# A row-wise L1 normalization: five places of ten rows in one SBUF tile, and one 40 KB packet per partition and transfer

## The chip, the core and the metric

The kernel runs on one core of one Trainium2 chip. The metric is the device time of one launch in microseconds (us). The kernel before was run three times: median 316.6 us, from 316.41 to 316.69.

## What is computed

```python
def reference(x):                       # x: 32 x 512 x 1024, float32
    sums = np.sum(np.abs(x), axis=-1, keepdims=True)
    return (x / (sums + 1e-8)).astype(np.float32)
```

Each of the 32 x 512 = 16,384 rows of 1024 numbers is divided by the sum of its absolute values. A row is 4 KB. The whole input is 67.11 MB and has to be read from HBM once; the output is as large and has to be written once.

## The kernel before, in words

The chip's SBUF has 128 partitions, so each partition gets 128 rows in all. The work is cut into eleven tiles: ten of 12 rows per partition and a last one of 8 (`rows`, line 31). Tiles 0, 1 and the last are cut out of the first 32 rows of each partition's share of the head of the input (`HEAD`, lines 33 to 38), so that their partitions lie 32 rows (128 KB) apart in HBM; the other tiles are contiguous blocks in which the partitions lie 12 rows (48 KB) apart. Within a partition the rows of a tile are always contiguous in HBM and in SBUF.

The program order is written out by hand (`manual_schedule`, lines 108 to 115). There are four buffers of 12 rows per partition (`BUFS`, line 42). Four loads are issued first. Then, for each tile in turn: compute it, store it, and issue the load that will reuse its buffer, four tiles further on.

- **load** (lines 85 to 87) is one DMA issued on SyncE's queue (SP; queue q1 in the profile). It waits until the store that used the buffer before has landed.
- **compute** (lines 45 to 73, 103 to 106): VectorE (DVE) sums the absolute values of each row (L47), adds 1e-8 (L54) and takes the reciprocal (L56). Then the rows are scaled in place: most of them by one VectorE multiplication with the reciprocals broadcast along the row (L58), some by one VectorE instruction per row (L65), some by one ScalarE (ACT) instruction per row (L68). The table `split` (line 76) says how many: of tile 0, five rows go to L58, three to L65 and four to ScalarE; tiles 1 and 2 give three rows to ScalarE, the last but one gives it two, and the last has four for L65 and four for ScalarE.
- **store** (lines 89 to 101) is one or two DMAs issued on ScalarE's queue (queue q10), in ScalarE's program order.

`max_dma_last_dim` sets the longest contiguous run, in bytes, that becomes one packet of a DMA. Each tile's rows of a partition are cut into such packets: 48 KB (`WHOLE`) for the loads of tiles 0 and 1 and for the stores of the last two tiles, 24 KB (`HALF`) for nearly everything else, so two packets per partition. The store of tile 0 is in two DMAs: three rows in packets of 4 KB, then nine rows in packets of 36 KB. The store of tile 8 is in two DMAs of six rows.

The core has 16 DMA engines, and both queues use all of them.

Of the kernel before, what the change touches and what calls it, by code (L numbers as in the profile page):

```python
# [1 line left out]

# [4 lines left out]

FP32 = mybir.dt.float32
EPS = 1e-8


@with_exitstack
def kernel(
    ctx: ExitStack,
    tc: tile.TileContext,
    x: bass.AP,
    out: bass.AP,
):
    nc = tc.nc
    P = nc.NUM_PARTITIONS  # L20

    x_flat = x.flatten_outer_dims()
    out_flat = out.flatten_outer_dims()
    n, d = x_flat.shape

    R = 12
    BUFS = 4
    HEAD = 32
    per_partition = n // P
    assert n % P == 0 and (per_partition - HEAD) % R == 0  # L30
    rows = [R] * ((per_partition - HEAD) // R + 2) + [HEAD - 2 * R]

    def piece(flat, i):
        head = flat[: P * HEAD, :].rearrange("(p r) d -> p r d", p=P)
        if i < 2:
            return head[:, R * i : R * (i + 1), :]
        if i == len(rows) - 1:
            return head[:, 2 * R :, :]
        a = P * (HEAD + R * (i - 2))
        return flat[a : a + P * R, :].rearrange("(p r) d -> p r d", p=P)  # L40

    sbuf = ctx.enter_context(tc.tile_pool(name="sbuf", bufs=BUFS))
    stats = ctx.enter_context(tc.tile_pool(name="stats", bufs=len(rows)))

    def normalize(x_tile, k, kv, kt):
        s = stats.tile([P, R], FP32)
        nc.vector.tensor_reduce(  # L47
            out=s[:, :k],
            in_=x_tile[:, :k, :],
            axis=mybir.AxisListType.X,  # L50
            op=mybir.AluOpType.add,
            apply_absolute_value=True,
        )
        nc.vector.tensor_scalar_add(out=s[:, :k], in0=s[:, :k], scalar1=EPS)  # L54
        inv = stats.tile([P, R], FP32)
        nc.vector.reciprocal(out=inv[:, :k], in_=s[:, :k])  # L56
        if kv:
            nc.vector.tensor_mul(  # L58
                out=x_tile[:, :kv, :],
                in0=x_tile[:, :kv, :],  # L60
                in1=inv[:, :kv].unsqueeze(2).to_broadcast([P, kv, d]),
            )
        for r in range(kv, kv + kt):
            row = x_tile[:, r, :]
            nc.vector.tensor_scalar_mul(out=row, in0=row, scalar1=inv[:, r : r + 1])  # L65
        for r in range(kv + kt, k):
            row = x_tile[:, r, :]
            nc.scalar.activation(  # L68
                out=row,
                in_=row,  # L70
                func=mybir.ActivationFunctionType.Copy,
                scale=inv[:, r : r + 1],
            )

    last = len(rows) - 1
    split = {0: (3, 4), 1: (0, 3), 2: (0, 3), last - 1: (0, 2), last: (4, 4)}

    tiles = {}

    HALF, WHOLE = 24576, 49152
    FIRST = 3

    def load(i):
        x_tile = tiles[i] = sbuf.tile([P, R, d], FP32, name="x_tile")
        nc.sync.dma_start(out=x_tile[:, : rows[i], :], in_=piece(x_flat, i), max_dma_last_dim=WHOLE if i < 2 else HALF)  # L87

    def store(i):
        if i == 0:  # L90
            parts = [(0, FIRST, 4 * d), (FIRST, R, WHOLE)]
        elif i == last - 2:
            parts = [(0, R // 2, HALF), (R // 2, R, HALF)]
        else:
            parts = [(0, rows[i], WHOLE if i >= last - 1 else HALF)]
        for a, b, size in parts:
            nc.scalar.dma_start(
                out=piece(out_flat, i)[:, a:b, :],
                in_=tiles[i][:, a:b, :],
                max_dma_last_dim=size,  # L100
            )

    def compute(i):
        k = rows[i]
        kt, ks = split.get(i, (0, 0))
        normalize(tiles[i], k, k - kt - ks, kt)

    with tc.manual_schedule():
        for i in range(BUFS):
            load(i)  # L110
        for i in range(len(rows)):
            compute(i)
            store(i)
            if i + BUFS < len(rows):
                load(i + BUFS)


# [1 line left out]
_INS = ['x']  # L119
_OUTS = [((32, 512, 1024), 'float32')]  # L120


# [23 lines left out]
```

## Time and profile before

| what | value |
|---|---|
| time, median of 3 runs | 316.6 us (316.41 to 316.69) |
| span of the profiled execution, first to last instruction | 315.2 us |
| what a run's time holds beyond that span (median less span) | 1.4 us |
| VectorE busy | 260.6 us, 83% of the span, 50 instructions |
| ScalarE busy | 18.5 us, 6% |
| bytes moved | 134.22 MB, mean 426 GB/s over the span |
| DMA packets | 5761 |

The profiled execution has no time of its own beside its span; 1.4 us is what launch and end add to it, by the median. "Busy" of a queue is the time that its packets took, summed over the 16 DMA engines and divided by 16 spans. Packets under 512 B are the markers, one per DMA and engine, that report a transfer's end. A packet's bytes and its time are counted where it begins, so the rate of a short window is uneven.

### The profile page before, as it was taken

The page shows a single profiled execution, that of the slowest core. Times are in us where ns is not written, and L with a number is a line of the kernel's source. Part 1 is how long each engine was busy: PE and PEld are TensorE (multiplying, and loading weights), DVE is VectorE, ACT ScalarE, POOL GpSimd, SP SyncE. Part 2 cuts the span into 40 slices and gives each one's busy share as a digit, 9 for nine tenths or more (in the row PEclk, how much of TensorE's full clock was granted, in tenths as well). Part 3 has the DMA queues.
Part 4 walks back from the last instruction along what each step waited for, and adds up shares of the span by engine and source line. Part 5 has one row for each costly group of instructions (what it writes and reads, how often), then busy time and mean ns, then how long its engine had stood idle before and what let it go on. Part 6 is the DMA issues. An engine that isn't in the chain of part 4 may idle for free.

```text
span 315.2 us, 172 instructions
## 1 busy us (share of the span) xinstructions
DVE 260.6 (83%) x50; ACT 18.5 (6%) x17; POOL 0.2 (0%) x4
## 2 busy tenths in 40 slices
DVE  0079999999999999989996997999699969999000
ACT  0010503004000000000000000000000000203200
POOL 0000000000000000000000000000000000000000
DMA  8999999999999999999999999999999999999997
GB/s 318 480 399 412 437 407 464 411 436 413 415 446 437 415 446 437 415 449 434 415 449 437 412 449 437 412 449 437 415 446 437 415 437 434 432 428 496 399 408 324
DMA packets 5761, 134.22 MB, mean 426 GB/s; under 512 B 385, under 2 KB 385, under 8 KB 769
## 3 DMA queue, kind: packets, MB, share of 16 engines
q1 hardware_dynamic: 2736, 67.11, 49.8%
q10 hardware_dynamic: 3024, 67.11, 49.4%
q14 instruction: 1, 0.00, 0.0%
HBM read 67.11 MB, written 67.11 MB: 426 GB/s over the span
## 4 chain that ended last, share of the span: by engine, by line
DVE 40%; DMA 33%; another core or an unknown queue 18%; ACT 1%; issue 0%; SPq 0%
DVE s L47 23%; DMA x_tile<-in_x_dram 17%; DMA out_dram<-x_tile 16%; DVE x_tile L58 15%; ACT x_tile L68 1%; DVE x_tile L65 1%; DVE inv L56 0%; DVE s L54 0%; SPq L87 0%
## 5 line engine op out<-in xcount | busy, mean ns | idle before, releaser
L47 DVE TENSOR_REDUCE s<-x_tile 128x12 f32<-128x12288 f32 (+1 forms) x11 | 138.2, 12562 | 29.8 <-DMA x_tile<-in_x_dram 29.8
L58 DVE TENSOR_TENSOR x_tile<-x_tile,inv 128x12288 f32<-128x12288 f32 (+3 forms) x10 | 113.6, 11358 | 0.5
L68 ACT ACTIVATE x_tile<-x_tile,inv 128x1024 f32<-128x1024 f32 x16 | 17.2, 1138 | 256.9 <-DVE inv L56 256.9
L65 DVE TENSOR_SCALAR x_tile<-x_tile,inv 128x1024 f32<-128x1024 f32 x7 | 4.8, 749 | 0.0
L56 DVE RECIPROCAL inv<-s 128x12 f32<-128x12 f32 (+1 forms) x11 | 2.5, 226 | 0.4
L68 ACT ACT_TABLE_LOAD x1 | 1.3, 1283 | 17.8 <-DMA x_tile<-in_x_dram 17.8
L54 DVE TENSOR_SCALAR s<-s 128x12 f32<-128x12 f32 (+1 forms) x11 | 1.9, 174 | 0.4
L130 POOL MEMSET const-bfloat16-1.0<- 128x1 bf16 x1 | 0.1, 101 | 0.0
L130 POOL MEMSET const-uint8-127<- 128x1 uint8 x1 | 0.1, 101 | 0.0
L130 POOL MEMSET const-float32-0.0<- 128x1 f32 x1 | 0.1, 98 | 0.2 <-issue 0.2
L130 POOL MEMSET const-float32-1.0<- 128x1 f32 x1 | 0.1, 98 | 0.0
## 6 DMA issues: line engine op xcount, KB each, us to landing
x_tile<-in_x_dram SPq DMA_DIRECT2D x10, 6144.0 KB, 36.9
out_dram<-x_tile ACTq DMA_DIRECT2D x8, 6144.0 KB, 49.1
out_dram<-x_tile ACTq DMA_DIRECT2D x2, 3072.0 KB, 33.4
out_dram<-x_tile ACTq DMA_DIRECT2D x1, 4608.0 KB, 37.9
x_tile<-in_x_dram SPq DMA_DIRECT2D x1, 4096.0 KB, 32.2
out_dram<-x_tile ACTq DMA_DIRECT2D x1, 4096.0 KB, 20.9
out_dram<-x_tile ACTq DMA_DIRECT2D x1, 1536.0 KB, 29.3
```

Source lines behind the costliest of these rows:

```text
L47: nc.vector.tensor_reduce(out=s[:, :k], in_=x_tile[:, :k, :], axis=mybir.AxisListType.X, op=mybir.AluOpType.add, apply_absolute_value=True,)
L54: nc.vector.tensor_scalar_add(out=s[:, :k], in0=s[:, :k], scalar1=EPS)
L56: nc.vector.reciprocal(out=inv[:, :k], in_=s[:, :k])
L58: nc.vector.tensor_mul(out=x_tile[:, :kv, :], in0=x_tile[:, :kv, :], in1=inv[:, :kv].unsqueeze(2).to_broadcast([P, kv, d]),)
L65: nc.vector.tensor_scalar_mul(out=row, in0=row, scalar1=inv[:, r : r + 1])
L68: nc.scalar.activation(out=row, in_=row, func=mybir.ActivationFunctionType.Copy, scale=inv[:, r : r + 1],)
L130: nc = _bacc.Bacc("TRN2", target_bir_lowering=False, num_devices=1)
```

## The change

- Tiles have 10 rows instead of 12 (twelve tiles of 10 and a last one of 8), all cut from the input in order; the head of 32 rows is gone.
- The buffers are five places of 10 rows in one tile `x_all` of 50 rows per partition, instead of four buffers of 12 rows. `cell(i, a, b)` names rows a to b of tile i's place. Five loads are issued first instead of four.
- `max_dma_last_dim` is 40,960 bytes for every DMA but one, so that each load and each store has one packet per partition (40 KB; 32 KB for the last tile). The exception is the first row of tile 0, stored by a DMA of its own in packets of 4 KB; the other nine rows follow in one of 36 KB packets.
- The scaling is split otherwise: VectorE's one multiplication takes all ten rows of tiles 1 to 11. ScalarE takes five rows of tile 0 and four of the last.

The diff, without the lines that only rename a tile (in `compute`, `x_tile[:, ...]` becomes `cell(i, ...)`):

```diff
-    R = 12
-    BUFS = 4
-    HEAD = 32
+    R, SLOTS = 10, 5
+    PACKET = 40960
     per_partition = n // P
-    rows = [R] * ((per_partition - HEAD) // R + 2) + [HEAD - 2 * R]
+    rows = [R] * (per_partition // R) + [per_partition % R] * (per_partition % R > 0)
+    last = len(rows) - 1
+    split = {0: (0, 5), last: (4, 4)}
 
     def piece(flat, i):
-        head = flat[: P * HEAD, :].rearrange("(p r) d -> p r d", p=P)
-        if i < 2:
-            return head[:, R * i : R * (i + 1), :]
-        if i == len(rows) - 1:
-            return head[:, 2 * R :, :]
-        a = P * (HEAD + R * (i - 2))
-        return flat[a : a + P * R, :].rearrange("(p r) d -> p r d", p=P)
+        a = P * R * i
+        return flat[a : a + P * rows[i], :].rearrange("(p r) d -> p r d", p=P)
 
-    sbuf = ctx.enter_context(tc.tile_pool(name="sbuf", bufs=BUFS))
+    sbuf = ctx.enter_context(tc.tile_pool(name="sbuf", bufs=1))
+    x_all = sbuf.tile([P, SLOTS * R, d], FP32, name="x_all")
+
+    def cell(i, a=0, b=None):
+        lo = R * (i % SLOTS)
+        return x_all[:, lo + a : lo + (rows[i] if b is None else b), :]
+
+    def load(i):
+        nc.sync.dma_start(out=cell(i), in_=piece(x_flat, i), max_dma_last_dim=PACKET)
+
+    def store(i):
+        parts = [(0, 1, 4 * d), (1, R, PACKET)] if i == 0 else [(0, rows[i], PACKET)]
+        for a, b, size in parts:
+            nc.scalar.dma_start(
+                out=piece(out_flat, i)[:, a:b, :],
+                in_=cell(i, a, b),
+                max_dma_last_dim=size,
+            )
...
-    split = {0: (3, 4), 1: (0, 3), 2: (0, 3), last - 1: (0, 2), last: (4, 4)}
-    HALF, WHOLE = 24576, 49152
-    FIRST = 3
...
     with tc.manual_schedule():
-        for i in range(BUFS):
+        for i in range(SLOTS):
             load(i)
         for i in range(len(rows)):
             compute(i)
             store(i)
-            if i + BUFS < len(rows):
-                load(i + BUFS)
+            if i + SLOTS < len(rows):
+                load(i + SLOTS)
```

More of the change, by code (lines that the diff above doesn't have):

```diff
@@ L24, with compute @@
     n, d = x_flat.shape
-    R = 12
-    BUFS = 4
-    HEAD = 32
+    R, SLOTS = 10, 5
+    PACKET = 40960
     per_partition = n // P
-    assert n % P == 0 and (per_partition - HEAD) % R == 0
-    rows = [R] * ((per_partition - HEAD) // R + 2) + [HEAD - 2 * R]
+    assert n % P == 0
+    rows = [R] * (per_partition // R) + [per_partition % R] * (per_partition % R > 0)
+    last = len(rows) - 1
+    split = {0: (0, 5), last: (4, 4)}
     def piece(flat, i):
-        head = flat[: P * HEAD, :].rearrange("(p r) d -> p r d", p=P)
-        if i < 2:
-            return head[:, R * i : R * (i + 1), :]
-        if i == len(rows) - 1:
-            return head[:, 2 * R :, :]
-        a = P * (HEAD + R * (i - 2))
-        return flat[a : a + P * R, :].rearrange("(p r) d -> p r d", p=P)
-    sbuf = ctx.enter_context(tc.tile_pool(name="sbuf", bufs=BUFS))
-    stats = ctx.enter_context(tc.tile_pool(name="stats", bufs=len(rows)))
-    def normalize(x_tile, k, kv, kt):
+        a = P * R * i
+        return flat[a : a + P * rows[i], :].rearrange("(p r) d -> p r d", p=P)
+    sbuf = ctx.enter_context(tc.tile_pool(name="sbuf", bufs=1))
+    stats = ctx.enter_context(tc.tile_pool(name="stats", bufs=len(rows)))
+    x_all = sbuf.tile([P, SLOTS * R, d], FP32, name="x_all")
[12 more added lines that the diff above has]
+            )
+    def compute(i):
+        k = rows[i]
+        kt, ks = split.get(i, (0, 0))
+        kv = k - kt - ks
         s = stats.tile([P, R], FP32)
@@ L48, in normalize @@
             out=s[:, :k],
-            in_=x_tile[:, :k, :],
+            in_=cell(i),
             axis=mybir.AxisListType.X,
@@ L58, in normalize @@
             nc.vector.tensor_mul(
-                out=x_tile[:, :kv, :],
-                in0=x_tile[:, :kv, :],
+                out=cell(i, 0, kv),
+                in0=cell(i, 0, kv),
                 in1=inv[:, :kv].unsqueeze(2).to_broadcast([P, kv, d]),
@@ L63, in normalize @@
         for r in range(kv, kv + kt):
-            row = x_tile[:, r, :]
+            row = cell(i, r, r + 1)[:, 0, :]
             nc.vector.tensor_scalar_mul(out=row, in0=row, scalar1=inv[:, r : r + 1])
         for r in range(kv + kt, k):
-            row = x_tile[:, r, :]
+            row = cell(i, r, r + 1)[:, 0, :]
             nc.scalar.activation(
@@ L73, in normalize @@
             )
-    last = len(rows) - 1
-    split = {0: (3, 4), 1: (0, 3), 2: (0, 3), last - 1: (0, 2), last: (4, 4)}
-    tiles = {}
-    HALF, WHOLE = 24576, 49152
-    FIRST = 3
[L85 to L106, printed above, removed]
     with tc.manual_schedule():
-        for i in range(BUFS):
+        for i in range(SLOTS):
             load(i)
```

## The prediction

> **What bounds it now.** I read the page first: not the shares of the engines, but the row of the DMA engines and the queues.
>
> ```profile
> DMA  8999999999999999999999999999999999999997
> DMA packets 5761, 134.22 MB, mean 426 GB/s; under 512 B 385, under 2 KB 385, under 8 KB 769
> q1 hardware_dynamic: 2736, 67.11, 49.8%
> q10 hardware_dynamic: 3024, 67.11, 49.4%
> ```
>
> The DMA engines are full from the second slice to the last but one. The two queues' packets take 49.8% + 49.4% = 99.2% of the span, 312.7 of 315.2 us; 2.5 us are left for both ends. VectorE's 83% hides idle time that costs nothing. The waits (engine, what it waited for: us in total, times, longest) say who waits for whom:
>
> ```profile
> DVE s L47 <- DMA x_tile<-in_x_dram: 29.8, 6, 17.8
> ```
>
> ```profile
> SPq L87 <- DMA out_dram<-x_tile: 242.1, 8, 63.3
> ```
>
> VectorE waits for loads (17.8 us for the first, then 1.4 to 2.7 us per tile), and SP waits for stores to free a buffer. Both ends of that circle are transfers. The chain of waits gives VectorE 40%, but that is one of several paths through full queues. So the time is: bytes at the rate of the packets, plus the two ends. Next the windows (the last two columns are the DMA share and GB/s):
>
> ```profile
> 66.00:80.00 14.00, 13.90 (x4) 3.23 (x3) 0.00 (x0) 1.00 1.00 434
> 84.00:250.00 166.00, 155.89 (x25) 0.00 (x0) 0.00 (x0) 1.00 1.01 433
> ```
>
> From 66 to 80 us the load queue is empty (load 4 is issued at 76.8 us, after waiting for store 0), and the store queue alone moves 434 GB/s. One queue with work is enough. A transfer that is issued earlier, or a deeper queue, gains nothing as long as either queue has packets.
>
> **The price of a packet.** The same stretches in the DMA view; a packet's mean time is share x window x 16 / packets, with the weightless markers (under 512 B) taken out of the count.
>
> ```profile
> DMA packets 254, 11.70 MB, mean 446 GB/s; under 512 B 16, under 2 KB 16, under 8 KB 16
> q1 hardware_dynamic: 254, 11.70, 103.1%
> ```
>
> This is 3.8 to 30 us, loads in 48 KB packets: 1.031 x 26.2 x 16 / 238 = 1815 ns each.
>
> ```profile
> DMA packets 3104, 71.96 MB, mean 433 GB/s; under 512 B 176, under 2 KB 176, under 8 KB 176
> q1 hardware_dynamic: 1552, 36.18, 50.6%
> q10 hardware_dynamic: 1552, 35.78, 50.0%
> ```
>
> This is 84 to 250 us, loads and stores in 24 KB packets: 1.006 x 166 x 16 / 2928 = 912.5 ns. From 41.5 to 61.5 us, the 320 packets of 4 KB take 15.9% of 20 us: 159 ns each. So 48 KB costs 1815 ns in one packet, 1825 in two, 1908 in twelve: (1908 - 1815) / 11 = 8.4 ns and 1825 - 1815 = 10 ns per packet beyond the bytes. The slope is (1815 - 159) / 45,056 B = 36.76 ns per 1000 B, so a 40 KB packet should take 159 + 36,864 x 0.03676 = 1514 ns.
>
> But packets also overlap a little: over three whole periods (160.35 to 247.62 us, the issues of load 7 and load 10) 1537 packets of 24 KB pass in 87.27 us, which is 908.5 ns of the clock each. By that the fixed part is as little as 2 x 908.5 - 1815 = 2 ns.
>
> **The change, part by part.**
>
> 1. *Packets.* Before: 5761 - 385 = 5376 data packets, 336 per DMA engine. After: 13 loads and 14 stores with one packet for each of 128 partitions, 27 x 8 = 216 per engine. 120 fewer, at 2 to 10 ns: **0.2 to 1.2 us** gained, all of it on the path, since the engines are never idle. Nearest to the new kernel is the steady stretch, where both queues alternate: there a 24 KB packet has 908.5 - 24,576 x 0.03676 = 5 ns beyond its bytes; the 48 KB loads alone have 8.4. I take 7: **0.84 us**. The Trainium skill ("DMA: Bandwidth & Descriptors", section "Why small descriptors are slow (HBM only)") gives a fixed ~3 cycles per packet, with 32 B moved per cycle; at 27.2 GB/s per engine that is 3.5 ns, an estimate from the page, and the sum would be a gain of 0.42 us. The rows contain this value and do not exclude it.
> 2. *4 KB packets* of the first store: 24 per engine become 8; counted above. Beside them the loads' packets ran a little long (86.2% of 20 us x 16 / 301 = 916.4 ns, 3.9 over): 0.07 us, of which two thirds go. **-0.05.**
> 3. *A stall at the end of the 4 KB phase.* From 62 to 64.8 us the last two load packets of every engine are slow:
>
> ```profile
> DMA packets 65, 0.92 MB, mean 329 GB/s; under 512 B 0, under 2 KB 0, under 8 KB 33
> q1 hardware_dynamic: 32, 0.79, 85.0%
> ```
>
>    0.850 x 2.8 x 16 / 32 = 1190 ns instead of 912.5, so 2 x 277 ns = **0.55 us** lost once. It stands where the store queue passes from 4 KB to 36 KB packets. The new kernel passes from 4 to 36 KB as well, a little earlier (about 47 us), so I leave it in: 0, with 0 to -0.6 for the range.
> 4. *Both ends.* The first packet of each engine takes 2.55 us (283.1% of 0.9 us x 16 / 16, in the window 1.6 to 2.5), 0.73 more than 1815 ns. It stays, as does the wait for the last store; the last store has the same 32 KB packets. 0.
> 5. *VectorE.* It loses ScalarE's help in tiles 1, 2 and 11. Per tile of ten rows: L47 10.8 us (between 12.95 for 12 rows and 8.69 for 8), L54 and L56 0.4, L58 10.8 (that row exists: 10.825), with gaps 22.1 us. The DMA needs 29.09 x 10/12 = 24.2 us for a tile's load and store. Tile 0 lands at about 15.4 us (17.8 less 8 packets x 0.30), and is scaled at 15.4 + 10.8 + 0.4 + 5.5 = 32. Then 11 x 22.1 and 13.4 for the last tile: its store is issued at about 289, and needs 8 x 1.21 + 2 = 12 us. It could be issued as late as about 302. Cost 0, with a cover of 13 us, 5% of VectorE's chain.
> 6. *Five places, ten rows.* At about 34 us store 0 enters; 8 rounds of 4 KB + 40 KB (13.4 us) and 8 of 36 + 40 KB (23 us) end it near 70, when load 5 is issued. The first 50 rows are read until about 80, so the load queue no longer runs dry; the row 66 to 80 says that this is worth nothing. The waits that the new order adds (on shared semaphores) are for transfers at least two tiles older, which have landed by then. 0.
> 7. *Three more DMAs*: 3 markers per engine, no weight.
>
> Sum: -0.84 - 0.05 = -0.9 us. The profiled span of 315.2 becomes 314.3; with the 1.4 us by which the median of the runs exceeds the span, **315.7 us**.
>
> **Rivals.**
> - *The stall goes too.* For: it is seen once, only where 4 KB packets end, and there will be 8 rounds of them instead of 24. Against: the same transition remains. 316.6 - 0.9 - 0.6 = **315.1**.
> - *The fixed part is hidden.* Packets overlap as in the three periods, at 2 to 3.5 ns each: gain 0.2 to 0.4, **316.3**. No change that can be measured: it can tell about 0.2%, 0.63 us. Fewer packets then don't do what they seem to. The skill's 3 cycles end here. For: 908.5 against 912.5. Against: 48 KB alone is at 434 GB/s, the mixed 24 KB at 433.
> - *Large packets disturb each other* (slower). No stretch of before has 36 KB or more from both queues at once. If an engine that writes a 40 KB store packet for 1.51 us leaves the next load packet's reads waiting, the loads run long, as at 62 us. Place: every alternation from 34 to 270 us. Price: 1 GB/s of the mixed rate is 236 / 433 = 0.54 us; the slowest mixed row (40 to 50 us, 424 GB/s, with 4 KB packets) would cost 9 x 0.54 = 4.9 and give about **320.6**. It decides from 1.6 GB/s on, where it eats the 0.9 us. Against: 24 KB packets alternate with no such loss. The same page of the Trainium skill ("Queues, rings and completion order") says that a DMA engine serves its queues in turn, a whole packet at a time; the even 50.6% and 50.0% agree.
>
> Beyond these, VectorE could be late by more than its 13 us of cover, or a place come free late; nothing in the rows points to it.
>
> **How the numbers follow.** Forecast 0.42, stall gone 0.25, fixed part hidden 0.18, disturbed 0.09, others 0.06. The range leaves out the last two (0.15) and little else: from 315.1 less the rest of a 10 ns price (0.36), 314.8, to the hidden case at its 2 ns end, 316.4, with 0.1 for the spread of the runs (316.41 to 316.69): 316.5. Faster by over 0.2% (below 315.97): all of the second case, 0.75 of the first, little of the third: 0.59. Within 0.2%: 0.28. Slower: 0.13.
>
> **What would show it.** Right: the DMA row stays at 9, 3456 data packets, 40 KB packets near 1514 ns, the steady rate at 433 to 434 GB/s; VectorE's wait for loads all but gone after the first tile, and the time no better for it. Wrong: slices of the DMA row under 9 in the middle; 40 KB packets above 1520 ns; a gap near 300 us, with VectorE last in the chain.

## The result, and the profile after

The changed kernel takes **318.7 us** (median of 4 runs, 318.64 to 319.08) against 316.6 (316.41 to 316.69): a ratio of 1.0070, 95% interval 1.0056 to 1.0084. It is 2.1 us slower; 0.9 us faster had been forecast, and the range ended at 316.5. The span of the profiled execution is 317.0 us.

In two experiments below (48 KB packets, and stores of 20 KB beside loads of 40 KB) the runs lie so far apart that the ratio leaves out those over 1.5% above the fastest; the spread is given beside it.

The page of the changed kernel, the lines that answer to those shown of before:

```profile
DMA  8999989999999999999999999999999899999994
...
DMA packets 3888, 134.22 MB, mean 423 GB/s; under 512 B 432, under 2 KB 432, under 8 KB 560
...
q1 hardware_dynamic: 1872, 67.11, 49.5%
q10 hardware_dynamic: 2016, 67.11, 49.0%
```

Packets are 3888 - 432 = 3456, as forecast. The queues' packets take 98.5% of 317.0 = 312.2 us: less than the 312.7 of before. So the DMA engines had a little *less* to do in a longer span. The row of slices says where the difference lies: only its last digit has changed clearly, from 7 to 4. (Two slices in the middle read 8, which the prediction had named as a sign of being wrong. A packet's time is counted where it begins: 245.7 to 253.6 us has 0.90, the next slice 1.03, and the steady stretch as a whole 1.00.) The waits:

```profile
DVE s L65 <- DMA x_all<-in_x_dram: 16.2, 1, 16.2
```

```profile
SPq L49 <- DMA out_dram<-x_all: 212.5, 9, 24.4
```

VectorE waits for one load, the first, and then never again, as forecast; the time is no better for it. The chain of waits, by engine, is misleading here:

```profile
DVE 81%; DMA 5%; issue 4%; ACT 1%; DVEq 0%
```

VectorE and ScalarE are done at 288.9 us, 28 us before the end. The chain follows busy engines back from the last instruction; that the transfers have been full all the while does not show in it.

Windows of the changed kernel (from:to, length, busy of VectorE, ScalarE and GpSimd, clock, then the DMA share and GB/s):

```profile
84.00:250.00 166.00, 165.18 (x32) 0.00 (x0) 0.00 (x0) 1.00 1.00 433
300.00:312.00 12.00, 0.00 (x0) 0.00 (x0) 0.00 (x0) 1.00 1.04 449
312.00:313.00 1.00, 0.00 (x0) 0.00 (x0) 0.00 (x0) 1.00 0.23 98
313.00:313.50 0.50, 0.00 (x0) 0.00 (x0) 0.00 (x0) 1.00 0.16 66
313.50:315.60 2.10, 0.00 (x0) 0.00 (x0) 0.00 (x0) 1.00 0.04 16
```

and the end of the kernel before:

```profile
312.00:313.00 1.00, 0.00 (x0) 0.00 (x0) 0.00 (x0) 1.00 1.21 524
313.00:313.50 0.50, 0.00 (x0) 0.00 (x0) 0.00 (x0) 1.00 0.01 0
313.50:315.20 1.70, 0.00 (x0) 0.00 (x0) 0.00 (x0) 1.00 0.00 0
```

A packet counts where it begins, so a share of 0.00 after 313.5 means that before begins no data packet there. The changed kernel does. The DMA view of 313.5 to 317 us names it:

```profile
DMA packets 3, 0.03 MB, mean 9 GB/s; under 512 B 2, under 2 KB 2, under 8 KB 2
...
q10 hardware_dynamic: 3, 0.03, 2.2%
```

One packet of 32 KB and two markers: **one DMA engine** still has a packet to move, of 0.022 x 3.5 x 16 = 1.23 us, when the others have stopped. Each DMA leaves one marker per engine, so the 16 markers of the last store, in order of time, tell when each engine is done: 14 lie between 312.9 and 313.3 us, one at 314.0, one at 315.5. In the kernel before all 16 lie between 313.3 and 313.8. The middle engine gained 0.4 us; the last lost 1.7, and the kernel ends with the last.

### The profile page after: what moved, and what is told of

Same layout as the page of the kernel before. It is cut to its first block, busy times and chain, and to the rows that moved or that the text cites. A ratio compares the mean times of both kernels' runs of the same rounds, so it can differ in the third digit from the quotient of the medians.

```text
span 317.0 us, 163 instructions
## 1 busy us (share of the span) xinstructions
DVE 269.8 (85%) x55; ACT 10.9 (3%) x10; POOL 0.2 (0%) x4
## 2 busy tenths in 40 slices
DMA packets 3888, 134.22 MB, mean 423 GB/s; under 512 B 432, under 2 KB 432, under 8 KB 560
## 4 chain that ended last, share of the span: by engine, by line
DVE 81%; DMA 5%; issue 4%; ACT 1%; DVEq 0%
DVE s L65 43%; DVE x_all L76 36%; DMA x_all<-in_x_dram 5%; DVE inv L74 1%; DVE s L72 1%; ACT x_all L86 1%; DVE x_all L83 0%; DVEq L126 0%
## 5 line engine op out<-in xcount | busy, mean ns | idle before, releaser
L65 DVE TENSOR_REDUCE s<-x_all 128x10 f32<-128x10240 f32 (+1 forms) x13 | 138.4, 10648 | 16.2 <-DMA x_all<-in_x_dram 16.2
L76 DVE TENSOR_TENSOR x_all<-x_all,inv 128x10240 f32<-128x10240 f32 (+1 forms) x12 | 124.6, 10381 | 0.4
L86 ACT ACTIVATE x_all<-x_all,inv 128x1024 f32<-128x1024 f32 x9 | 9.6, 1138 | 261.8 <-DVE inv L74 261.8
L74 DVE RECIPROCAL inv<-s 128x10 f32<-128x10 f32 (+1 forms) x13 | 2.8, 215 | 0.4
L83 DVE TENSOR_SCALAR x_all<-x_all,inv 128x1024 f32<-128x1024 f32 x4 | 2.7, 748 | 0.0
L72 DVE TENSOR_SCALAR s<-s 128x10 f32<-128x10 f32 (+1 forms) x13 | 2.3, 173 | 0.5
```

The source lines that it names most:

```text
L65: nc.vector.tensor_reduce(out=s[:, :k], in_=cell(i), axis=mybir.AxisListType.X, op=mybir.AluOpType.add, apply_absolute_value=True,)
L76: nc.vector.tensor_mul(out=cell(i, 0, kv), in0=cell(i, 0, kv), in1=inv[:, :kv].unsqueeze(2).to_broadcast([P, kv, d]),)
L86: nc.scalar.activation(out=row, in_=row, func=mybir.ActivationFunctionType.Copy, scale=inv[:, r : r + 1],)
```

## The experiments

The theory after the result: the sum for a typical engine was nearly right, and one engine that falls behind sets the time. Its rivals are what might make it fall behind: the passage from 4 KB to large packets (B), large packets on two queues (A), or something in the new layout (C). The "lead" is the rows of the first store that go ahead in 4 KB packets. Ordinary fences with "last less middle" come from the markers of one DMA: how far the last engine is behind the middle one.

**First: lead and packet sizes.** `e1_no_lead`, on the changed kernel:

```diff
-        parts = [(0, 1, 4 * d), (1, R, PACKET)] if i == 0 else [(0, rows[i], PACKET)]
+        parts = [(0, rows[i], PACKET)]
```

> The changed kernel with the first store whole, in one DMA of 40 KB packets; no 4 KB packets at all. In the changed kernel's trace 14 or 15 of the 16 DMA engines are done at about 313.2 us, earlier than before; one goes on to 315.5, and the time is that one's. All engines lose about 0.8 us once, at 49 us, where the store queue passes from 4 KB to 36 KB packets. Theory A (the 40 KB packets of both queues, alternating, make one engine fall behind): the 0.8 us stall may go, the straggler of some 2 us stays, 317.9 to 318.7. Theory B (the passage from small to large packets makes the stall and throws one engine out of step): both go, 315.3 to 316. Theory C (places, row count, or the start of five loads): about 318 to 318.7.

Measured: 319.0 us (ratio 1.0074, 1.0059 to 1.0089), last engine 2.6 us behind the middle one. Theory B falls: the late engine needs no 4 KB packets, and neither does the stall of the first store, which is 1.1 us here, at 36 us.

`e2_half` (`PACKET = 20480`, the first store as it was):

> The changed kernel with 20 KB packets, two per partition, for all loads and all stores but the first, whose lead of 4 KB and rest of 36 KB stay. Theory A (large packets on both queues): no engine falls behind, about 316.5. Theory B (passage from 4 to 36 KB): the stall and the straggler stay, 318.5 to 319.5, packets of 20 KB costing about 1 us more. Theory C (places, rows, five loads): 318.5 to 319.5 too.

Measured: 317.9 us (1.0042, 1.0027 to 1.0057). The last engine is 0.9 us behind at tile 0 and 1.0 at the end: the start is as late, but nothing is added. Of the 1.3 us over before, 0.7 are that engine's and some 0.4 are 80 packets more per engine (at the 4.6 ns measured below).

`e3_before_whole`, on the kernel before:

```diff
-    HALF, WHOLE = 24576, 49152
+    HALF, WHOLE = 49152, 49152
```

> The kernel before with 48 KB packets wherever it had 24 KB; four buffers of 12 rows, the three-row lead in 4 KB packets and the order stay. Theory A (large packets on both queues): one engine falls behind, 318 to 319.5. Theory B (passage from 4 KB to large packets): the stall at the end of the 4 KB phase is there as it was, or longer with longer load packets; 315.8 to 317. Theory C: 315.7, as forecast for fewer packets.

Measured: ten runs from **316.1 to 322.4 us** (1.004, 1.0013 to 1.0067). Three of the ten (316.14, 316.25, 316.33) are faster than every run of the kernel before beside them (316.40 to 316.74). The profiled one took 321.0: its engines start even (0.15 us), then three fall behind, the last by 5.1. At the markers around 76 us the last is 0.34 us behind, at those of load 4 (111.6 us) 2.95, and the losses go on until about 280 us. So large packets are what makes engines part, without a late start too: theory A, but as a risk, not a fixed price. That the three quickest runs gain their 0.3 us because their engines kept together is likely, but no trace of them was kept.

`e4_loads_half` (`max_dma_last_dim=PACKET // 2` for loads alone) and its mirror image `e8_stores_half` (the same for all stores but the first):

> The changed kernel with 20 KB packets for the loads alone; stores keep 40 KB, the first its 4 KB lead. Theory A: if the load packets' size is what lets an engine fall behind, about 316.5; if the stores' size is, 318.5. Theory B: the stall at the end of the 4 KB phase shrinks with the load packet (0.55 us with 24 KB, 0.8 with 40 KB): about 316.5 to 318. Theory C: 318.5.

> The changed kernel with 20 KB packets for all stores but the first, and 40 KB for the loads: the mirror image of the run with halved load packets, which took 326.7 us. If the DMA engines serve the queues in turn, a packet each, the loads now have two thirds of the rate while both queues have work and stores are late instead of loads. A place then comes free late, the load queue runs dry by turns and the stores catch up; nothing is left to starve at the end: 317.5 to 320. If the 326.7 came from unequal sizes as such (stalls at every change of size) and not from the order in which work is done: about 326 again.

Measured: 326.7 us (1.0332, 1.0311 to 1.0353; 325.9 to 327.9) and 327.5 us (1.0325, 1.0289 to 1.0360; 325.4 to 330.8), 8 to 10 us slower than either size alone on both queues. With small load packets a store lands sooner (the second store DMA at 62 us instead of 73 in the changed kernel) and loads come later: VectorE waits for ten of them, 38.5 us in all, and from 294 to 312 us the DMA share is 0.75. That is what serving the queues in turn, a packet each, does to the queue with the smaller packets; the Trainium skill ("DMA: Bandwidth & Descriptors", section "Queues, rings and completion order") has this rule, and the trace agrees: from 46 to 58 us, 95 load packets of 20 KB begin beside 91 store packets of 36 KB, 1.95 MB against 3.35. The mirror image was misjudged: nothing starves, but one engine falls 10 us behind. Its windows:

```profile
300.00:313.50 13.50, 0.00 (x0) 0.00 (x0) 0.00 (x0) 1.00 1.00 430
313.50:325.60 12.10, 0.00 (x0) 0.00 (x0) 0.00 (x0) 1.00 0.11 48
```

A share of 0.11 for 12 us is not quite two engines of sixteen in the mean: by the markers of the last store, one engine is busy until 324.2 us and three more until 316.4 to 317.5, the plainest picture of late engines in this study.

`e7_rows8_32k`: tiles of 8 rows, six places, 32 KB packets.

> The changed kernel with tiles of 8 rows, six places of 8 rows and packets of 32 KB (one per partition); lead of one row as there, four rows of tile 0 by ScalarE. If engines fall behind by degrees with the packet's size: the last engine between 0.5 us (24 KB) and 2.4 us (40 KB) behind, 317 to 318. If there is a limit between 24 and 32 KB: 318.5. If the limit lies between 32 and 40 KB: 316 to 316.6.

Measured: 317.15 us (1.0022, 1.0012 to 1.0032), nine runs from 316.7 to 318.0. This lies between the times for 24 KB (316.4 to 316.7) and 40 KB, as "by degrees" expected, but it does not show it. The engines start even here (0.27 us) and end 0.63 apart, and 40 KB packets with an even start take less (316.75, under "Fifth").

**Second: is it the marker, or the two queues?** In the changed kernel the late engine loses its time in single packets. This is the DMA view of 96.7 to 97.05 us, in which only that engine begins a packet, right behind the marker of a store:

```profile
DMA packets 2, 0.04 MB, mean 117 GB/s; under 512 B 1, under 2 KB 1, under 8 KB 1
...
q1 hardware_dynamic: 1, 0.04, 35.9%
q10 hardware_dynamic: 1, 0.00, 0.2%
```

0.359 x 0.35 x 16 = 2.01 us for a load packet that takes 1.514 elsewhere. The same happens to it behind the markers of the next two stores (2.00 us at 121.5, 1.90 at 146.2). The three cost 1.4 us; with the 1.2 that it is behind at tile 0 already, this is its distance at the end. The engines that run together lose nothing at theirs. Nor does every late engine: the second latest is 0.94 us behind the middle one at the markers around 152 us and 0.93 at the end.

`e5_more_markers`: each store as two DMAs of 64 partitions (`for h in (0, 64)` around the issue, `[h : h + 64]` on both sides).

> The changed kernel with each store cut into two DMAs of 64 partitions; packet sizes, bytes and order stay, and each store ends in two sets of markers instead of one. In the changed kernel's trace the late DMA engine loses 0.4 to 0.5 us at a time, each time on the load packet that follows right behind the marker of a store (96.8, 121.5 and 146.2 us), while the engines that run in step lose nothing there. Theory M (an engine out of step loses time at each marker of a store): twice as many such places, the last engine 3 to 5 us behind the others, 320 to 322. Theory N (the loss has to do with the end of a whole tile, or with the engine itself, not with the marker): 318.5 to 319.

Measured: 382.9 to 395.4 us, far outside all expectations, and it decides nothing about markers. The edit changed more than their number: a DMA of 64 partitions has four packets for each engine where a load has eight, ScalarE's queue now waits between the halves of a store (issues at 174.6 and 184.4 us, for one), and the rate in the steady stretch falls from 433 to 373 GB/s. A badly chosen experiment.

`e9_one_queue` and `e10_one_queue_half` (the latter with 20 KB packets):

```diff
-            nc.scalar.dma_start(
+            nc.sync.dma_start(
...
-            if i + SLOTS < len(rows):
-                load(i + SLOTS)
+            if i and i - 1 + SLOTS < len(rows):
+                load(i - 1 + SLOTS)
```

> The changed kernel with its stores issued on SP's queue too, so that all transfers stand in one queue; after each store, SP issues the load of the place that the store before it frees (one tile later than in the changed kernel). Packets of 40 KB, places and engines' work stay. Runs so far: with 40 or 48 KB packets on two queues the DMA engines that are out of step fall further behind, up to 2.5 and 5 us; with 20 and 24 KB they keep their distance. Theory A (it needs large packets of two queues that take turns): in one queue the last engine keeps the distance that it has at the start (about 1 us), the others are done at about 313, so 316.5 to 317. Theory E (the engine is slower with large packets in any order): 318 to 319.5. If the one queue runs dry because SP waits in order, slices of the DMA row under 9 will show it, and the time is above 319.

> The same single queue with 20 KB packets. Against the single queue with 40 KB packets this tells whether one queue or the packet's size matters: 200 packets per engine more at 3 to 5 ns are 0.6 to 1 us. Theory A: that much slower than the single queue with 40 KB, 317.1 to 318. Theory E: faster than the single queue with 40 KB, as 20 KB are faster than 40 KB on two queues (317.9 against 318.7).

Measured: 321.2 us (1.0149, 1.0132 to 1.0166) and 322.3 us (1.0178, 1.0163 to 1.0193). The queue never ran dry. The end of the first, 313.5 to 319.5 us:

```profile
DMA  0000009500000050000000500000000000000000
...
q1 hardware_dynamic: 9, 0.16, 6.4%
```

Nine packets begin in 6 us, of which four are markers: a few engines left over. Theory A falls in its narrow form: it needs no two queues, and in one queue 20 KB packets don't help either. What the markers show (40 KB; only loads and stores in turn from here on):

```
DMA          store 1   load 5   store 2   load 6   store 3   load 7   store 4   load 8
last less    1.88      2.67     2.67      2.67     2.67      3.19     3.19      3.43   us
middle
```

In this stretch the last engine loses only in loads, 0.2 to 0.8 us at a time, and never in a store. But here it is not the packet behind a store's marker. The loss in load 5 is one packet that begins at 99.2 us and takes 2.30 us (33.4% of 0.43 us x 16, from 99.17 to 99.6 us, in which no other packet begins). The last marker of store 1 lies at 90.15, six packets earlier; the other engines pass from load 5 to store 2 while that packet runs (their markers lie between 100.06 and 100.66). So the two cases share only that a late engine loses in single load packets. On two queues with 20 or 24 KB packets the last engine's distance grows by 0.1 to 0.2 us over the whole kernel (`e2_half`, and `f1_before_no_head` below). Why, no run here shows.

**Third: the price of a packet.** `e11_before_16k`: the kernel before with `HALF = 16384`.

> The kernel before with 16 KB packets wherever it had 24 KB: 472 data packets per engine instead of 336, and nothing else changed. This measures the price of a packet on the path, without an engine that falls behind. At 2 ns per packet 316.9, at 5 ns 317.3, at 7 ns (the value in the prediction) 317.5, at 10 ns 318.

Measured: 317.45 us (1.0027, 1.0018 to 1.0037; 317.0 to 318.2), engines even (last less middle 0.2 at both ends). Its steady stretch against the 433 GB/s of both others:

```profile
84.00:250.00 166.00, 155.79 (x25) 0.00 (x0) 0.00 (x0) 1.00 1.01 431
```

The sharpest figure is the period of the load issues, divided by the packets of one engine in it: 607 ns for 16 KB (29.16 us, 48 packets), 909 for 24 KB (29.08 us, 32), 1512 for 40 KB (24.19 us, 16). The line through them is 36.8 ns per 1000 B and **4.6 ns per packet**. 120 packets are 0.55 us. By its whole time this run would give more, 0.88 us for 136 packets or 6.5 ns each; but its stall at the first store is longer as well: from 57 to 60.2 us its 45 load packets take 916 ns each instead of 611 (80.5% of 3.2 us x 16 / 45), 0.86 us per engine against 0.55 in the kernel before.

**Fourth: the stall at the first store.** `e6_before_lead5`: the kernel before with `FIRST = 5`.

> The kernel before with five rows of the first store in 4 KB packets instead of three. In its trace the load queue's last two packets per engine are slow (1190 ns instead of 912, 0.55 us in all) just before the 36 KB store packets begin. Theory S (that stall belongs to the moment when large store packets join a load queue that still has work): five rows of 4 KB packets outlast the first four loads, the large packets begin when the load queue is dry, the stall is gone: 316.0 to 316.2. Theory T (the stall belongs to the passage from small to large packets as such, or to that time): it stays, 316.6 to 316.8.

Measured: 316.6 us (1.0002, 0.9993 to 1.0011). Large store packets begin at 67.2 us, after the load queue has run dry at 65; the load's last two packets are slow all the same, at 62 us, by 0.2 us each. Theory S falls as it was put.

**Fifth: the late start.** The longest wait of VectorE for a load is the first, and it ends when the *last* engine has brought tile 0. In every run with ten rows and partitions 40 KB apart it is 15.8 to 16.2 us; before's 17.8 less 8 x 0.30 for the smaller packets should be 15.4. In the changed kernel's trace one engine alone begins its first packet after 2.3 us; this is the DMA view from 2.3 to 3.4 us:

```profile
DMA packets 1, 0.04 MB, mean 37 GB/s; under 512 B 0, under 2 KB 0, under 8 KB 0
...
q1 hardware_dynamic: 1, 0.04, 15.3%
```

That packet takes 0.153 x 1.1 x 16 = 2.69 us; the mean of all 16 first packets is 2.25 (125.2% of 1.8 us x 16 / 16, from 1.6 to 3.4 us). `e12_head`, on the changed kernel:

```diff
+    HEAD = 38
...
-        a = P * R * i
-        return flat[a : a + P * rows[i], :].rearrange("(p r) d -> p r d", p=P)
+        head = flat[: P * HEAD, :].rearrange("(p r) d -> p r d", p=P)
+        if i < 3:
+            return head[:, R * i : R * (i + 1), :]
+        if i == last:
+            return head[:, 3 * R :, :]
+        a = P * (HEAD + R * (i - 3))
+        return flat[a : a + P * R, :].rearrange("(p r) d -> p r d", p=P)
```

`f2_head20` has `HEAD = 20` and only tiles 0 and 1 in it. `f1_before_no_head` takes the head out of the kernel before (`a = P * R * i` for all tiles).

> The changed kernel with tiles 0, 1, 2 and the last cut out of the first 38 rows of each partition's share, as the kernel before does with 32, so that their partitions lie 152 KB apart in HBM instead of 40 KB. In the six runs that read the first tile with partitions 40 KB apart, the last engine ends tile 0 0.8 to 1.2 us after the middle one; in the four runs with 128 KB or 32 KB it is 0.15 to 0.3 us. Theory L (the distance in HBM makes the late start, and the late engine then falls back further): no late start, and the time falls to 316.0 to 317, or is spread as with 48 KB packets (316.1 to 322). Theory F (the late start comes from the five loads or the packet's size): still 0.8 to 1.2 us at tile 0, 318.5 to 319.

> The kernel before without its head: all tiles cut from the input in order, so that the partitions of tiles 0, 1 and the last lie 48 KB (32 KB) apart in HBM instead of 128 KB; rows, buffers, packets and order stay. Theory L (a short distance between partitions makes one engine start late): at tile 0 the last engine is 0.8 to 1.2 us behind the middle one instead of 0.3, and since 24 KB packets on two queues let it keep its distance, the time is 317.2 to 317.6. If the late start belongs to 40 KB alone: 316.6, and the last engine within 0.4 us at tile 0.

> The changed kernel with a head of 20 rows: tiles 0 and 1 have their partitions 80 KB apart, all others as in the changed kernel. Theory L, the distance decides by being short: no late start, 316.5 to 317.2, as with 152 KB. If the head's other effect decides (that tiles 0, 1, 2 and the last lie in one stretch of HBM) or if 80 KB is as bad as its half: late start of 0.8 to 1.2 us at tile 0, 318.3 to 319.

Measured: `e12_head` **316.75 us** (1.0006, 0.9996 to 1.0015; 316.55 to 317.01), `f2_head20` 316.8 (1.0011, 1.0000 to 1.0021; 316.5 to 317.9, three of its ten runs at 317.3 or more), `f1_before_no_head` 317.2 (1.0021, 1.0010 to 1.0031; 317.0 to 317.9). VectorE's waits, of `e12_head`:

```profile
DVE s L71 <- DMA x_all<-in_x_dram: 15.6, 1, 15.6
```

and of `f1_before_no_head`, against before's 17.8:

```profile
DVE s L42 <- DMA x_tile<-in_x_dram: 30.7, 6, 18.4
```

In `e12_head` two engines begin their first packets between 2.3 and 3.4 us, and these take 0.200 x 1.1 x 16 / 2 = 1.76 us each:

```profile
q1 hardware_dynamic: 2, 0.08, 20.0%
```

The end of `e12_head`, where no engine is left over:

```profile
312.00:313.00 1.00, 0.00 (x0) 0.00 (x0) 0.00 (x0) 1.00 0.53 229
313.00:313.50 0.50, 0.00 (x0) 0.00 (x0) 0.00 (x0) 1.00 0.02 0
```

Theory L holds in all three: partitions of tile 0 that lie 80, 128 or 152 KB apart start even, 40 and 48 KB start one engine late, in two kernels and both ways. (32 KB, with eight rows, started even as well, so "short" is not the whole rule. Why the distance matters, no run shows; the markers are of one traced run per kernel.)

```
kernel              partitions of   last less middle, us     time, us
                    tile 0 apart    tile 0    last store
before              128 KB          0.30      0.34           316.6
f1_before_no_head    48 KB          0.82      1.02           317.2
changed              40 KB          1.17      2.47           318.7
f2_head20            80 KB          0.35      0.34           316.8
e12_head            152 KB          0.42      0.26           316.75
e3_before_whole     128 KB          0.15      5.13           316.1 to 322.4
```

`f3_head_lead3` is `e12_head` with three rows in 4 KB packets ahead of the first store.

> The changed kernel with the head of 38 rows (316.75 us, no late start) and three rows instead of one in 4 KB packets at the front of the first store. The one stall left, where the first store joins the loads, was 0.8 us with one row (40 KB load packets), and 0.55 and 0.47 with three and five rows in the kernel before (24 KB). If more 4 KB rows shorten it: 316.3 to 316.6, at or below the kernel before. If the stall goes with the load packet's size: 316.7 to 317.

Measured: 319.4 us (1.0085, 1.0068 to 1.0103), against both expectations. The start is even. The three rows last until the first loads are done, the load queue is dry at 67 us, and when load 5 joins the store queue at 80 us, packets of 40 KB run long on nearly every engine until 97 us; two engines come out of it some 2.5 us late and end 2.9 and 3.0 us behind the middle one. The passage that cost before nothing (it has one at 80 us, with 24 KB packets) is a place where engines part with large ones, an even start or not. In `e3_before_whole`, which has the same passage with 48 KB packets, the first large loss lies between the markers at 76 and 112 us.

No run beats both kernels: `e12_head` equals before, and only the three quickest runs of `e3_before_whole` lie below it.

## Why the prediction was wrong, point by point

- **What bounds the kernel** was read rightly: the DMA engines are full, VectorE's 85% and its vanished waits are worth nothing (steps 5 and 6: no waits after the first, last store issued at 288.95 against "about 289", load 5 at 75.9 against "near 70").
- **Step 1, packets**: right in kind. 40 KB packets took 1514 ns, to the nanosecond of the interpolation, and by the periods of the load issues the steady rate rose from 432.7 to 433.5 GB/s. The size was 0.84 us for 120 packets at 7 ns; measured 4.6 ns, 0.55 us. The Trainium skill's 3 cycles (3.5 ns, an estimate from "DMA: Bandwidth & Descriptors", section "Why small descriptors are slow (HBM only)") are below the measured 4.6, the value taken is above.
- **Step 3, the stall** was left at 0.55 us. It comes at 49 us and costs one load packet per engine 2.34 us instead of 1.51 (334.5% of 0.7 us x 16 / 16), 0.83 us: **+0.3**, as the load packet is longer. The rival in which it goes was wrong.
- **Step 4, "both ends", priced at 0, is the step that failed.** "The first packet of each engine takes 2.55 us ... It stays" is a mean over 16 engines. The mean did stay: 0.74 us over a normal packet after the change, 0.73 before. But the sum treated the engines as one, and the kernel ends with its last engine: 2.5 us behind the middle one instead of 0.3, **+2.1**. Of this, 0.9 us are there at tile 0 (1.17 less 0.30), which is this step. Some 1.3 come later, in single load packets of that one engine; for them the sum has no term. The part of the change that brings it, tiles cut from the input in order, has no step in the prediction at all; the head looked like bookkeeping, and is what starts the engines of the kernel before evenly. With it put back, 2.0 of the 2.1 us are gone, the later losses included.
- The sum with the measured terms: 315.2 - 0.55 + 0.3 + 2.1 = 317.05, against a measured span of 317.0. Outside the span lie 1.6 us in the changed kernel's runs, and also 1.6 in the later runs of before (316.5 to 316.6 at spans of 314.9): the profile of before was 0.2 to 0.3 us longer than its usual run.
- **The slower rival** expected loads of the mixed stretch to run long and the rate to fall. The rate did not: 433 GB/s, 1514 ns. Its bare statement, that large packets cost something that 24 KB packets don't, was right, but by another way: they let single engines fall back.
- That `e12_head` gains nothing on the kernel before, though 0.55 us of packets are saved and only 0.3 are given back in the stall, is not resolved. The two traces do differ by this much (314.9 against 315.2), but the one is the quickest of its ten runs and the other a long one; its runs vary by 0.5 us, those of before beside it by 0.9.

## What to carry to other kernels

Where the DMA engines are full, ask for the slowest of the 16, not for their mean: look at the last slices and at the markers of the first and the last transfer before trusting a sum of packet times. The gain from larger packets is small here (0.55 us, 0.2%, by the price of a packet), no run shows it clear of the noise, and one late engine undoes it: in these runs 20 and 24 KB on both queues keep a late engine at its distance, 40 and 48 KB can let it fall back. Keep packet sizes equal on queues that share the engines, and treat the address pattern of the very first load as part of the tuning.

## What the runs showed that had not been expected

- In these runs the distance between the partitions of the first tile in HBM decides how evenly the 16 DMA engines begin: 0.15 to 0.5 us from middle to last at 80, 128 and 152 KB (and 32 KB), 0.8 to 1.2 us at 40 and 48 KB.
- With 20 KB packets on one queue and 40 KB on the other the kernel is 8 to 10 us slower than with either on both.
- A store in two halves of 64 partitions each, beside loads of 128, takes 383 to 395 us instead of 318.7.
